# Gate and up products of an FFN by seven products of quarter blocks instead of eight, with precomputed weight sums and a serial background queue

## The chip, the cores and the metric

The kernel runs on one core of one Trainium2 chip. The metric is the device time of one execution in microseconds. The engines are TensorE (PE: matmuls and, as PEld, its weight loads), VectorE (DVE), ScalarE (ACT), GpSimd (POOL) and SyncE (SP, which here only issues DMAs).

## The reference

One inference step of one decoder layer with two parallel head groups, for a prompt of 2048 tokens with 16 meta tokens ahead of it and 8 running sequences of 8 new tokens each (64 sample tokens). Cut to what matters:

```
z = x @ w_in                       # q, k, v, conv path c, mLSTM v, output gate, input/forget gates
att = sliding-window attention(q, k, v)          # window 128, 8 query heads, 2 KV heads, sinks, ALiBi
h_m = mLSTM(silu(causal_conv(c)), ...)           # 4 heads of 128, chunk by chunk of 128 tokens
y   = concat([head_norm(att), head_norm(sigmoid(o_pre) * h_m)])
x1  = layer_norm(alpha * x + y @ w_out)          # 1024 features
ffn = (silu(x1 @ w_gate) * (x1 @ w_up)) @ w_down # 1024 -> 2816 -> 1024
out = layer_norm(alpha * x1 + ffn)
```

Besides the outputs y for prompt and sample tokens, the last keys and values, the conv state and the mLSTM state are returned. All data are float32.

## The kernel before, in words

Activations lie with features on the 128 partitions and tokens along the columns, so a product of a 128x128 weight block with up to 512 token columns is one matmul. To keep float32 accuracy at the faster matmul type, every operand is split into a rounded part and a remainder (`split`, lines 117 to 120: ACT rounds, line 111; DVE or Pool subtracts, line 120), and a product is three matmuls (`mm3`, lines 122 to 125: high by high, high by low, low by high).

The work has three stages. **First input projection** (lines 182 to 300): 17 token tiles times three column ranges of `w1a`, the results by tokens, stored to DRAM as `TM` and `TMS`. **Second input projection** (lines 904 to 992): five token groups of 424 or 426 columns times nine output tiles of `w1b` (six in the last group), convolution and the q/k maps, stored to DRAM as `FM`. **FFN stage** (lines 995 to 1248): five token groups of 384, 440, 440, 440 and 408 columns (`FF_GROUPS`). Of each group: the output projection `out_proj` (8 output tiles of 8 k-blocks), layer norm `ln1` with the split of its result into `x1`, then 22 feed-forward tiles of 128 features in `SLICES` of 5, 5, 6 and 6: for each tile `gate_up` (lines 1142 to 1161) makes two products of 8 k-blocks, gate and up, each in a PSUM bank of its own; ACT takes the tanh from the gate's bank, DVE makes t from it and multiplies with the up bank, and the result is split into `hh` and `hl`. After each slice `down` (lines 1163 to 1176) adds the slice's 8 output tiles to z. The next group's output projection and `ln1` stand within the last slice, `ln2` within the next group's first tiles.

Weights are loaded again for each group by `wtile` (line 998): SP loads 512 KB, ACT rounds, DVE (or Pool, one in eight of those with 8 k-blocks) subtracts. `wnext` keeps three ahead. Raw, high and low come in turn from one ring of 8 tiles of 1024 columns (`wpl`, line 151), so that the load of one waits until the ring comes round.

**Background.** Attention and mLSTM of the 16 prompt chunks, and of the sample tokens, are generators (`bg_attn`, line 484; `bg_ml`, line 628; `bg_sample_attn`, `bg_sample_ml`) that yield after each small step. A queue (lines 845 to 852) holds one entry for each chunk; `both` (line 835) takes one step of attention and one of mLSTM at a time, 12 double steps a chunk. `pace` gives out steps between the main products at a rate that brings a group's chunks to an end before its output projection needs them (`need`), and `bg_drain` runs what is left.

PSUM has eight banks: three for the main products (`gps`, line 75) and five for the background (`bps`, line 78).

What is written in this order is not the order of the engines: the kernel is built with `schedule_with_timeline_sim=True` (line 1347), where each engine's instructions are put in an order at build, by when their operands would be ready and by their place in the program. On the chip each engine then runs its list in that order.

Of the kernel before, what the change touches and what calls it, by code (L numbers as in the profile page):

```python
# [17 lines left out]
KD = 8  # L18
# [21 lines left out]
FF_GROUPS = [384, 440, 440, 440, 408]  # L40
FW = max(FF_GROUPS)
XW = max(IN_GROUPS + FF_GROUPS)
SLICES = [5, 5, 6, 6]
NLATE = 3
CZ = 3

# [3 lines left out]
def tile_hymba(  # L50
# [15 lines left out]

    cp = ctx.enter_context(tc.tile_pool(name="const", bufs=1))
# [4 lines left out]
    pg = ctx.enter_context(tc.tile_pool(name="pg", bufs=3, space=bass.MemoryType.PSUM))  # L72
    pb = ctx.enter_context(tc.tile_pool(name="pb", bufs=5, space=bass.MemoryType.PSUM))

    def gps(shape=None):
        return pg.tile(shape or [128, 512], F32, tag="g", name="gps")

    def bps(shape=None):
        return pb.tile(shape or [128, 512], F32, tag="b", name="bps")
# [42 lines left out]
    def mm3(out, wh, wl, xh, xl, start, stop):  # L122
        PE.matmul(out, lhsT=wh, rhs=xh, start=start, stop=False)  # L123
        PE.matmul(out, lhsT=wh, rhs=xl, start=False, stop=False)  # L124
        PE.matmul(out, lhsT=wl, rhs=xh, start=False, stop=stop)  # L125
# [25 lines left out]
    wpl = ctx.enter_context(tc.tile_pool(name="wpl", bufs=8, reuse_waits="tile"))  # L151
    xpl = ctx.enter_context(tc.tile_pool(name="xpl", bufs=22, reuse_waits="tile"))

    def w_tile(dt=F32R):
        return wpl.tile([128, KD, 128], dt, tag="w", name="w")

    def x_tile(dt=F32R):
        return xpl.tile([128, XW], dt, tag="x", name="x")

    def load_w(i):  # L160
        m = MT[i]
        if i < NEARLY:
            raw = ep.tile([128, KD, 128], F32, tag="wbr", name="wbr", bufs=1)
            hi, lo = w_tile(), w_tile()
        else:
            raw = b1["w"].tile([128, KD, 128], F32, tag="wbr", name="wbr", bufs=1)
            hi = b1["w"].tile([128, KD, 128], F32R, name=f"wbh{m}")
            lo = b1["w"].tile([128, KD, 128], F32R, name=f"wbl{m}")
        SP.dma_start(out=raw, in_=w1b[:, m, :].rearrange("p (k j) -> p k j", j=128))
        split("p" if i % 2 else "a", hi, lo, raw)  # L170
        wbh[m], wbl[m] = hi, lo
# [10 lines left out]
    with ExitStack() as s1:  # L182
        wp = s1.enter_context(tc.tile_pool(name="w1a", bufs=1, reuse_waits="tile"))
# [44 lines left out]
        start = [[f() for _ in CUT] for f in (gps, bps)]  # L228
# [14 lines left out]
        for i in range(NCH + 1):  # L243
# [11 lines left out]
            else:  # L255
                ps = []
                for c0, w in CUT:
                    xh, xl, n = xs[i]
                    p = (gps if flip[0] % 8 < 3 else bps)()
                    flip[0] += 1  # L260
# [4 lines left out]
            pa, pbk, pc = ps  # L265
            st = tp.tile([128, TMW], F32, tag="st", name="st", bufs=2)
# [36 lines left out]
    def gates():  # L303
# [35 lines left out]
        b = bps()  # L339
        PE.matmul(b[:, 0:NC4], lhsT=U, rhs=lf[:, 0:NC4], start=True, stop=True)  # L340
        bs = bps()
        PE.matmul(bs[0:NS, 0:4], lhsT=Us, rhs=lf[0:NS, sl], start=True, stop=True)
        bT = bps()
        PE.matmul(bT[0:NC4, 0:128], lhsT=lf[:, 0:NC4], rhs=U, start=True, stop=True)
        bTs = bps()
# [8 lines left out]
        aTs = bps()  # L354
# [112 lines left out]
    def att_rstd(o, w):  # L467

        sq = t2k("pt", [128, 512], 4)
        A.activation(out=sq[:, 0:w], in_=o[:, 0:w], func=AF.Square)  # L470
        sh, sl = (t2k("pt", [128, 512], 4, F32R) for _ in range(2))
# [5 lines left out]
        ve = t2k("pt", [128, 512], 4)  # L477
        V.tensor_scalar(out=ve[:, 0:w], in0=var[:, 0:w], scalar1=EPS, scalar2=None, op0=ALU.add)
        ry, tt = (t2k("pt", [128, 512], 4) for _ in range(2))
# [4 lines left out]
    def bg_attn(c):  # L484
# [19 lines left out]
        Pt = t2k("P", [128, 8, 256], 1)  # L504
# [30 lines left out]
        o = bps()  # L535
        halves = [(0, npv, 0), (nk - 128, 128, 1)]
        for c0, n, j in halves:
            ps = []
            for g in range(2):
# [3 lines left out]
                p = t2k("pt", [128, 512], 4)  # L543
# [60 lines left out]
    def bg_meta():  # L604
        km = t2k("fm", [128, 4, 128], 2)
        vm = t2k("vmo", [128, 4, 129], 1)
# [10 lines left out]
        S = t2k("S", [128, 4, 129], 2)  # L617
# [10 lines left out]
    def bg_ml(c):  # L628
# [4 lines left out]
        gw = t2k("gw", [128, 4, 2, 128], 1)  # L633
        vmo = t2k("vmo", [128, 1028], 1)
# [11 lines left out]
        gm = t2k("gm", [128, 4, 128], 1)  # L646
        G.affine_select(out=gm, in_=gw[:, :, 0, :], pattern=[[0, 4], [1, 128]], compare_op=ALU.is_ge,
# [8 lines left out]
        for h in range(4):  # L656
# [5 lines left out]
        V.tensor_tensor(out=gm.rearrange("p h t -> p (h t)"), in0=gm.rearrange("p h t -> p (h t)"), in1=sc,  # L662
                        op=ALU.mult)
        yield
        S = state["S"]
        Sn = t2k("S", [128, 4, 129], 2)
        nd = []
        for j in range(2):
            u = bps()
# [4 lines left out]
            for hh in range(2):  # L674
                h = 2 * j + hh
                V.scalar_tensor_tensor(out=Sn[:, h, :], in0=S[:, h, :], scalar=DEC[:, r0 + h:r0 + h + 1],
                                       in1=u[:, 129 * hh:129 * hh + 129], op0=ALU.mult, op1=ALU.add)
            yield
            x = bps([128, 2, 256])
            for hh in range(2):  # L680
                h = 2 * j + hh
                PE.matmul(x[:, hh, 0:129], lhsT=qs[:, h, :], rhs=S[:, h, :], start=True, stop=False)  # L682
                PE.matmul(x[:, hh, 0:129], lhsT=gm[:, h, :], rhs=vm[:, h, :], start=False, stop=True)
            nd.append(x[:, :, 0:129])
            yield
        state["S"] = Sn
        if c == NCH - 1:
            SP.dma_start(out=pS, in_=Sn)
        yield from mlstm_tail(nd, 128, ENM[:, r0:r0 + 4], o, 128 * c)

    def bg_sample_attn():
# [9 lines left out]
        o = bps()  # L701
        yield
        for hf in range(2):
# [10 lines left out]
            for g in range(2):  # L714
                pr = slice(64 * g, 64 * g + 64)
                tb = t2k("pt", [128, 192], 4)
# [6 lines left out]
                X = t2k("P", [128, 192], 1)  # L723
# [21 lines left out]
                ps = t2k("pt", [128, 256], 4)  # L745
# [22 lines left out]
    def bg_sample_ml():  # L768
        qm = t2k("fm", [128, 4, NS], 2)
        km = t2k("fm", [128, 4, NS], 2)  # L770
        sg = t2k("gw", [128, 4, 136], 1)
        vmo = t2k("vmo", [128, 1028], 1)
# [4 lines left out]
        SP.dma_start(out=vmo[0:NS], in_=TMS[0:NS, 128:TMW])  # L777
        vm = vmo[:, 0:516].rearrange("p (h e) -> p h e", h=4)
        o = vmo[:, 516:1028]
# [5 lines left out]
        gm = t2k("gm", [128, 4, NS], 1)  # L785
# [18 lines left out]
        nd = [bps([128, 2, 256]) for _ in range(2)]  # L804
        for h in range(4):
            pp = t2k("P", [128, 2, 8, 129], 1)
# [563 lines left out]
```

## Time and profile before

| what | us |
|---|---|
| median of 3 runs | 2508.75 (2508.75 to 2509.66) |
| the profiled execution | 2508.94 |
| its span, first to last instruction | 2507.1 |
| PE busy | 2444.7 |
| PEld busy (weight loads, beside PE) | 2267.2 |
| DVE busy | 1514.9 |
| ACT busy | 955.3 |
| POOL busy | 328.3 |

The mean granted TensorE clock was 0.989 of full speed. From the places of the first matmuls of each kind in the trace, the first input projection runs to 226 us, the second to 504 us, and the FFN stage from there to the end. How to read the lines: a group of instructions is `line engine operation out<-in shape xcount | busy us, mean ns of one | idle time of the engine before them, and what ended it`. In the order of time a line is `start us, us, engine line operation, out<-in, shape, count`; equal neighbours are merged. In the table of stretches each line gives busy time and count of PE, PEld, DVE, ACT and POOL, then the granted clock, the share of the DMA engines and GB/s. A matmul's record lasts until its result is written, and records of neighbours overlap; the step from one start to the next tells what a matmul costs.

### The profile page before, as it was taken

The page shows a single profiled execution, that of the slowest core. Times are in us where ns is not written, and L with a number is a line of the kernel's source. Part 1 is how long each engine was busy: PE and PEld are TensorE (multiplying, and loading weights), DVE is VectorE, ACT ScalarE, POOL GpSimd, SP SyncE. Part 2 cuts the span into 40 slices and gives each one's busy share as a digit, 9 for nine tenths or more (in the row PEclk, how much of TensorE's full clock was granted, in tenths as well). Part 3 has the DMA queues.
Part 4 walks back from the last instruction along what each step waited for, and adds up shares of the span by engine and source line. Part 5 has one row for each costly group of instructions (what it writes and reads, how often), then busy time and mean ns, then how long its engine had stood idle before and what let it go on. Part 6 is the DMA issues. An engine that isn't in the chain of part 4 may idle for free.

```text
span 2507.1 us, 34929 instructions
## 1 busy us (share of the span) xinstructions
PE 2444.7 (98%) x13135; PEld 2267.2 (90%) x13135; DVE 1514.9 (60%) x3129; ACT 955.3 (38%) x1730; POOL 328.3 (13%) x253
## 2 busy tenths in 40 slices
PE   8999999889999999999999999999999999999997
PEld 8999888788989989888999899989899999999997
DVE  6214466457786888656674976666775434764444
ACT  3112444335433444324333543343343323443332
POOL 1000000021000014210011500100420000420001
PEclk9999999998999999999999999999999999999998
DMA  7222534563444543554343353433344333343342
GB/s 234 89 90 85 173 119 131 132 207 117 144 130 126 160 146 94 175 159 144 120 137 121 106 188 122 140 119 107 109 142 133 117 111 121 104 143 114 118 127 77
DMA packets 197330, 327.89 MB, mean 131 GB/s; under 512 B 31010, under 2 KB 133498, under 8 KB 197146
## 3 DMA queue, kind: packets, MB, share of 16 engines
q1 hardware_dynamic: 170400, 294.29, 38.7%
q10 hardware_dynamic: 26762, 31.36, 3.6%
q8 instruction: 104, 1.70, 0.3%
q14 instruction: 64, 0.52, 0.1%
HBM read 281.59 MB, written 44.99 MB: 130 GB/s over the span
## 4 chain that ended last, share of the span: by engine, by line
PE 88%; DVE 4%; DMA 4%; ACT 1%; issue 1%; POOL 0%; SPq 0%; ACTq 0%; DVEq 0%; POOLq 0%
PE gps L123 25%; PE gps L125 24%; PE gps L124 24%; PE bps L123 2%; PE bps L125 2%; PE bps L124 2%; DMA w<-in_wo 1%; PE bps L513 1%; PE bps L549 1%; PE bps L542 1%; PE gps L937 1%; DVE w L120 1%; PE bps L682 1%; PE bps L655 1%; PE bps L672 1%
## 5 line engine op out<-in xcount | busy, mean ns | idle before, releaser
L123 PE MATMUL gps<-x,w 128*128 128x440 f32 (+4 forms) x2240 | 792.3, 358 | 11.1 <-DVE z L1075 5.6
L125 PE MATMUL gps<-x,w 128*128 128x440 f32 (+4 forms) x2240 | 797.9, 357 | 3.4 <-POOL w L120 2.7
L124 PE MATMUL gps<-x,w 128*128 128x440 f32 (+4 forms) x2240 | 794.0, 356 | 0.6 <-DVE x L1122 0.6
L111 ACT CAST w<-w 128x1024 fp32r<-128x1024 f32 (+2 forms) x423 | 400.6, 947 | 775.2 <-DMA w<-in_wd 271.8
L120 DVE TENSOR_TENSOR w<-w 128x1024 fp32r<-128x1024 f32 (+2 forms) x391 | 441.5, 1130 | 359.7 <-ACT w L111 185.4
L123 PEld LDWEIGHTS gps<-x,w 128*128 128x128 f32 x2240 | 422.4, 189 | 36.5 <-DVE z L1075 7.4
L125 PEld LDWEIGHTS gps<-x,w 128*128 128x128 f32 x2240 | 422.6, 189 | 23.3 <-POOL w L120 4.4
L124 PEld LDWEIGHTS gps<-x,w 128*128 128x128 f32 x2240 | 422.6, 189 | 18.4 <-DVE x L1122 0.9
L123 PE MATMUL gps<-hh,w 128*128 128x440 f32 (+2 forms) x880 | 314.8, 362 | 1.4 <-DVE z L1172 1.3
L125 PE MATMUL gps<-hh,w 128*128 128x440 f32 (+2 forms) x880 | 313.1, 357 | 0.0
L124 PE MATMUL gps<-hl,w 128*128 128x440 f32 (+2 forms) x880 | 312.5, 356 | 0.0
L123 PEld LDWEIGHTS gps<-hh,w 128*128 128x128 f32 x880 | 166.1, 189 | 11.9 <-issue 4.6
L124 PEld LDWEIGHTS gps<-hl,w 128*128 128x128 f32 x880 | 166.3, 189 | 8.1 <-issue 1.5
L125 PEld LDWEIGHTS gps<-hh,w 128*128 128x128 f32 x880 | 166.1, 189 | 7.4 <-issue 0.5
L120 POOL TENSOR_TENSOR w<-w 128x1024 fp32r<-128x1024 f32 x32 | 77.4, 2419 | 727.1 <-ACT w L111 475.2
L1172 DVE SCALAR_TENSOR_TENSOR z<-z,gps 128x440 f32<-128x440 f32 (+2 forms) x160 | 93.0, 589 | 69.1 <-PE gps L125 68.7
L111 ACT CAST hh<-hr 128x440 fp32r<-128x440 f32 (+2 forms) x110 | 60.0, 545 | 165.2 <-DVE hr L1158 165.0
L1158 DVE SCALAR_TENSOR_TENSOR hr<-ft,gps 128x440 f32<-128x440 f32 (+2 forms) x110 | 64.9, 590 | 81.3 <-PE gps L125 81.0
L1155 ACT ACTIVATE ft<-gps 128x440 f32<-128x440 f32 (+2 forms) x110 | 57.4, 522 | 113.1 <-PE gps L125 112.6
L120 DVE TENSOR_TENSOR hl<-hr,hh 128x440 fp32r<-128x440 f32 (+2 forms) x110 | 83.8, 762 | 27.6 <-ACT hh L111 27.3
L1066 POOL TENSOR_TENSOR zs<-zs,z 128x440 f32<-128x440 f32 (+2 forms) x58 | 80.0, 1379 | 102.0 <-DVE z L1075 66.3
L1156 DVE SCALAR_TENSOR_TENSOR ft<-ft,gps 128x440 f32<-128x440 f32 (+2 forms) x110 | 64.7, 588 | 46.4 <-ACT ft L1155 46.3
(338 smaller groups left out, 3111.0 us busy)
## 6 DMA issues: line engine op xcount, KB each, us to landing
w<-in_wg SPq DMA_DIRECT2D x110, 512.0 KB, 3.5
w<-in_wu SPq DMA_DIRECT2D x110, 512.0 KB, 3.5
w<-in_wd SPq DMA_DIRECT2D x80, 384.0 KB, 3.1
w<-in_wd SPq DMA_DIRECT2D x80, 320.0 KB, 2.9
w<-in_wo SPq DMA_DIRECT2D x40, 512.0 KB, 3.7
FM<-ev ACTq DMA_DIRECT2D x52, 213.0 KB, 1.9
TM<-st ACTq DMA_DIRECT2D x16, 578.0 KB, 3.7
vmo<-TM SPq DMA_DIRECT2D x16, 514.0 KB, 3.4
```

The costliest lines, as they stand in the source:

```text
L111: A.copy(out, src)
L120: return veng.tensor_tensor(out=lo, in0=src, in1=hi.bitcast(F32), op=ALU.subtract)
L123: PE.matmul(out, lhsT=wh, rhs=xh, start=start, stop=False)
L124: PE.matmul(out, lhsT=wh, rhs=xl, start=False, stop=False)
L125: PE.matmul(out, lhsT=wl, rhs=xh, start=False, stop=stop)
L513: PE.matmul(s[g][:, j, 0:nk], lhsT=x[r, 2 * tt + j, :], rhs=y[r, 0:nk], start=(i == 0), stop=(i == 2))
L542: PE.transpose(pt[0:n, 128 * t:128 * t + 128], Pt[:, 4 * g + t, c0:c0 + n], ident)
L1066: G.tensor_tensor(out=s[:, 0:w], in0=s[:, 0:w], in1=z[m][:, 0:w], op=ALU.add)
L1155: A.activation(out=t[:, 0:w], in_=pgt[:, 0:w], func=AF.Tanh, scale=0.5)
L1156: V.scalar_tensor_tensor(out=t[:, 0:w], in0=t[:, 0:w], scalar=1.0, in1=pgt[:, 0:w], op0=ALU.add, op1=ALU.mult)
L1158: V.scalar_tensor_tensor(out=hr[:, 0:w], in0=t[:, 0:w], scalar=0.5, in1=pu[:, 0:w], op0=ALU.mult, op1=ALU.mult)
L1172: V.scalar_tensor_tensor(out=zm, in0=zm, scalar=ALPHA if s == 0 else 1.0, in1=p[:, 0:w], op0=ALU.mult, op1=ALU.add)
```

## The change

**Gate and up.** The token groups become four pairs of half groups: `WH = [256, 256, 272, 272]`, so pairs of 512, 512, 544 and 544 columns (`W2`). For a pair of neighbouring feed-forward tiles (11 pairs) and for each of the two weights the product is that of a 2x2 block matrix A (two output tiles by two halves of k, each block 128 outputs by 4 k-blocks) with a 2x2 block matrix B (two halves of k by two half groups). It is made of seven products instead of eight, in the Winograd form of Strassen's scheme:

```
PROD = {"P1": ("A11", "B11"), "P2": ("A12", "B21"), "P3": ("S4", "B22"), "P4": ("A22", "T4"),
        "P5": ("S1", "T1"), "P6": ("S2", "T2"), "P7": ("S3", "T3")}
```

Each product is 4 k-blocks times three matmuls, 256 or 272 columns wide. S1 to S4 are sums of weight blocks, T1 to T4 sums of the blocks of x1. P6, P7 and P4 add onto P1's bank after it has been read, and P3 onto P5's:

```
if name == "P1":   A.copy(c1[:, a], p)
elif name == "P2": V.tensor_tensor(out=c1[:, a], in0=c1[:, a], in1=p, op=ALU.add)
elif name == "P6": A.copy(c1[:, b], p)
elif name == "P7": A.copy(c2[:, b], p)
                   V.tensor_tensor(out=c2[:, b], in0=c2[:, b], in1=S["ga"][:, a], op=ALU.add)
elif name == "P3": V.tensor_tensor(out=c1[:, b], in0=c1[:, b], in1=p, op=ALU.add); gated(S, 0)
elif name == "P4": A.copy(c2[:, a], p); gated(S, 1)
```

The order is, with P3 and P4 taken from the product set before: P1, P2, P3 (before), P6, P4 (before), P5, P7. P1's bank has two buffers, P2's and P5's one each. c1 and c2 lie in SBUF; `gated` takes tanh and products from there, at the full pair's width, and splits the result.

**Weight sums.** S1 to S4 of all 22 pairs are made once, in the two input-projection stages, and stored to a DRAM tensor `SW`; the FFN loads them from there for each group:

```
def sums(pool):
    for mt, src in enumerate((wg, wu)):
        for q in range(NPAIR):
            for o in (0, 256):
                a = ...tile([128, 2, 2, 256], F32, tag="sa", bufs=1); t = ...tile([128, 4, 256], F32, tag="st4", bufs=1)
                SP.dma_start(out=a, in_=src[:, 2*q:2*q+2, :]...[:, :, :, o:o + 256])
                for i, (x, y, op) in enumerate(...):       # four of them
                    G.tensor_tensor(out=t[:, i], in0=x, in1=y, op=op)
                A.dma_start(out=SW[:, NPAIR * mt + q, :, o:o + 256], in_=t)
                yield
```

There are 44 such steps. One follows each tile from the third on in the first stage (15), and each output tile in the second until they are used up (29).

**Sums of x1.** `ln1` now makes seven split operands of half the features and half the columns: B11, B21, T2, T1, T3, B22, T4. T1 and T3 are subtracted by Pool, T2 and T4 by DVE; the remainders of B22 and T4 are made by Pool.

**Weights of the FFN.** All come in blocks of 4 k-blocks (256 KB): for a group 154 for gate and up, 16 for the output projection, 48 for down (8 of them of 2 k-blocks). The ring has `NWB = 17` tiles of 512 columns; `LOOK = 5` blocks are asked for ahead. One in four (`WP = 4`) has its remainder made by Pool. `SLICES` is 4, 4, 4, 4, 6.

**Down and output projection** take 512 columns at once, or 544 as two of 272. In the last group `down` of the last slice goes over the first half and then the second, and each half has its own `ln2`.

**PSUM and background.** Four banks (tags ga twice, gb, gc) serve the main products, two `b` and two `bo` the background. `both` gives way to `chain`: attention of a chunk, then its mLSTM, 19 single steps; mLSTM now makes its outputs from the state before it updates the state in place, and several work tiles share one buffer `P`. As the first pair needs 512 tokens, four chunks instead of three have to be done before the FFN stage. Steps are given out after each of the seven products; while a group's `ln2` runs, a step of it is taken after P3 and P5 instead.

```
-        queue.append((e, e, 12, both(bg_attn(c), bg_ml(c))))
+        queue.append((e, e, 19, chain(bg_attn(c), bg_ml(c))))
```

**Small things.** The conv state of the sample tokens is loaded and stored in one DMA each by SP instead of four each on ACT's queue; late tiles of q are written through another buffer; the buffers for temporaries are renumbered (`FTB = 7`, `PTB = 3`).

More of the change, by code (lines that the diff above doesn't have):

```diff
@@ L39 @@
 IN_GROUPS = [426, 426, 426, 426, 424]
[L40 to L43, printed above, removed]
+WH = [256, 256, 272, 272]
+W2 = [2 * w for w in WH]
+F0 = [sum(W2[:i]) for i in range(len(W2))]
+HW = max(WH)
+FW = 2 * HW
+SLICES = [4, 4, 4, 4, 6]
+NPAIR = NFF // 2
 NLATE = 3
 CZ = 3
+NWB = 17
+PTB = 3
+FTB = 7
+LOOK = 5
+WP = 4
+NFIRST = 12
+LSTEP = [2, 1, 1, 1, 1, 1, 2, 2]
 @with_exitstack
@@ new lines, in ln2 @@
+        def ln2(g, cc, fast=False):
+            z = P[g]["z"]
+            for c in cc:
+                ry = yield from norm(z, c, P[g]["zs"], bps, fast)
+                for k in range(KD):
+                    scale(z, k, c, ry, Q_L2G)
+                    A.activation(out=z[k][:, c], in_=z[k][:, c], func=AF.Identity,
+                                 bias=Q[:, Q_L2B + k:Q_L2B + k + 1])
+                    (SP if fast else A).dma_start(out=yT[:, k, F0[g] + c.start:F0[g] + c.stop], in_=z[k][:, c])
+                    if k == KD // 2 - 1 and not fast:
+                        yield
+                yield
@@ new lines, in tile_hymba, with after, down, fn @@
+        pend, rate = [None], [0.0]
+        def after(name):
+            if pend[0] is not None:
+                if name in ("P3", "P5") and next(pend[0], 0) == 0:
+                    pend[0] = None
+            else:
+                pace(rate[0])
+        def down(g, s, m, cc, zs, adds, then=None):
+            j0, n = sum(SLICES[:s]), SLICES[s]
+            parts = [(k, min(4, n - k)) for k in range(0, n, 4)]
+            def fn(*wb):
+                z, h = P[g]["z"], P[g]["h"][:n]
+                for c in cc:
+                    p = gps()[:, 0:c.stop - c.start]
+                    for (k, nn), w in zip(parts, wb):
+                        product(p, w, [(hh[:, c], hl[:, c]) for hh, hl in h[k:k + nn]], k == 0, k + nn == n)
+                    zm = z[m][:, c]
+                    V.scalar_tensor_tensor(out=zm, in0=zm, scalar=ALPHA if s == 0 else 1.0, in1=p,
+                                           op0=ALU.mult, op1=ALU.add)
+                    if zs and m < adds:
+                        add_to(P[g]["zs"], z, m, c)
+                if then is None:
+                    pace(rate[0])
+                else:
+                    then()
+            item(fn, *[(wd[:, m, 128 * (j0 + k):128 * (j0 + k + nn)], nn) for k, nn in parts])
@@ L1252, in _consts @@
+        run()
 def _consts():
```

623 lines of the change are left out of this document (362 added, 261 removed).

## The prediction

> **What bounds the kernel now.** I read the page's first and fourth parts, then busy time by stage, then single matmuls in the order of time, then the groups of instructions by shape.
>
> ```profile
> span 2507.1 us, 34929 instructions
> PE 2444.7 (98%) x13135; PEld 2267.2 (90%) x13135; DVE 1514.9 (60%) x3129; ACT 955.3 (38%) x1730; POOL 328.3 (13%) x253
> ...
> PE 88%; DVE 4%; DMA 4%; ACT 1%; issue 1%; POOL 0%; SPq 0%; ACTq 0%; DVEq 0%; POOLq 0%
> ```
>
> TensorE is busy 98% of the span and makes 88% of the chain that ended last; it is idle for 2507.1 - 2444.7 = 62 us in all. A change that takes matmul time away is worth that time, as long as no other engine becomes late. Busy time by stage (the two input-projection stages, then the FFN stage from 504 us), and in two stretches of 100 us:
>
> ```profile
> 0.00:226.00 226.00, 219.34 (x1224) 215.69 (x1225) 72.23 (x172) 51.05 (x90) 23.72 (x42) 1.00 0.39 128
> 226.00:504.00 278.00, 269.79 (x1414) 234.91 (x1412) 163.58 (x453) 125.81 (x287) 11.70 (x12) 0.99 0.48 136
> 504.00:2507.00 2003.00, 1955.57 (x10501) 1816.63 (x10500) 1279.08 (x2505) 778.41 (x1354) 292.88 (x199) 0.99 0.42 130
> ...
> 800.00:900.00 100.00, 99.91 (x605) 92.24 (x605) 82.01 (x216) 46.94 (x102) 8.99 (x6) 1.00 0.50 153
> 1400.00:1500.00 100.00, 98.76 (x533) 88.24 (x532) 84.34 (x171) 52.36 (x101) 24.43 (x18) 1.00 0.47 152
> ```
>
> The columns are PE, PEld, DVE, ACT, POOL, then the granted clock (0.99 to 1.00: no throttle to win back) and DMA. In the FFN stage DVE is busy 1279 of 2003 us. Where it is busiest, 82 and 84 of 100 us, TensorE still reaches 99.9 and 98.8: up to there DVE does not hold it.
>
> **TensorE's part of the change.** What a matmul costs is its step to the next one, since records overlap. Steps at 440, 384 and 408 columns, then a run of score matmuls at 256 columns and one of 128:
>
> ```profile
> 1900.04 0.37 PE L125 MATMUL gps<-x,w 128*128 128x440 f32 x1
> ...
> 1902.44 0.36 PE L125 MATMUL gps<-x,w 128*128 128x440 f32 x1
> ```
> ```profile
> 640.13 0.34 PE L125 MATMUL gps<-hh,w 128*128 128x384 f32 x1
> ...
> 641.70 0.34 PE L125 MATMUL gps<-hh,w 128*128 128x384 f32 x1
> ```
> ```profile
> 2250.00 0.35 PE L124 MATMUL gps<-hl,w 128*128 128x408 f32 x1
> ...
> 2251.85 0.35 PE L125 MATMUL gps<-hh,w 128*128 128x408 f32 x1
> ```
> ```profile
> 1134.59 0.98 PE L513 MATMUL bps<-kt,qt 64*128 64x256 f32 x12
> 1134.82 0.52 PE L513 MATMUL bps<-kt,qt 64*128 64x256 f32 x6
> ...
> 1135.29 0.28 PE L513 MATMUL bps<-kt,qt 64*128 64x256 f32 x2
> ```
> ```profile
> 1135.82 0.39 PE L655 MATMUL bps<-fm 128*128 128x128 f32 x2
> ...
> 1136.16 0.50 PE L655 MATMUL bps<-fm 128*128 128x128 f32 x3
> ```
>
> Twelve steps at 440 columns take 2.40 us: 200 ns. Nine at 384 take 1.57: 174. Ten at 408 take 1.85: 185. So a column costs 26/56 = 0.46 ns. The score matmuls run as pairs in the two halves of the rows; after the first, four steps take 1135.29 - 1134.82 = 0.47 us, 118 ns with a new weight load each; I take 119 for the view's rounding. At 272 columns that is 119 + 16 x 0.46 = 126. The L655 run (128 columns, two passes of an exact float32) steps at 0.34/3 = 113 with a full 128x128 load each: a load that nothing hides better cannot be much longer than that.
>
> Gate and up before: 22 tiles x 2 matrices x 8 k x 3 = 1056 matmuls a group, so 1056 x (174 + 3 x 200 + 185) ns = 1013 us. After: 11 pairs x 2 x 7 products x 4 k x 3 = 1848 a group, two groups at 256 and two at 272: 3696 x (119 + 126) ns = 906 us. **Term: -107 us.** Seven products for eight alone would be -127; the rest is that short matmuls cost 0.465 ns a column for 0.455. Bounds of the step: 113 (the L655 load) gives 3696 x (113 + 120) = 861, 45 us better; 119 + 12 = 131 gives 995, where the term is nearly gone.
>
> Down and output projection keep their matmuls, 528 + 192 = 720 a group: before 720 x 959 ns = 690 us. After, at 512 columns 200 + 72 x 0.46 = 233 ns, and 544 as two of 272: 720 x 2 x (233 + 252) = 698. **Term: +8.** Background matmuls, the late tiles and the norms stay, one background chunk moving from the FFN stage into the second input stage; both stages are TensorE's, so that is nothing in sum.
>
> **What lies beside it.** Rows for the other engines, by shape:
>
> ```profile
> L120 DVE TENSOR_TENSOR w<-w 128x1024 fp32r<-128x1024 f32 x231 | 292.0, 1265 | 195.1 <-ACT w L111 131.7 <-PE gps L124 37.0 <-issue 14.3
> L120 DVE TENSOR_TENSOR w<-w 128x768 fp32r<-128x768 f32 x80 | 83.5, 1043 | 92.9 <-PE gps L124 60.5 <-ACT w L111 26.3 <-issue 3.2
> L120 DVE TENSOR_TENSOR w<-w 128x640 fp32r<-128x640 f32 x80 | 66.0, 826 | 71.8 <-PE gps L124 36.0 <-ACT w L111 27.5 <-issue 5.4
> ...
> L120 DVE TENSOR_TENSOR hl<-hr,hh 128x440 fp32r<-128x440 f32 x66 | 50.2, 761 | 17.0 <-ACT hh L111 16.6
> ...
> L136 DVE SCALAR_TENSOR_TENSOR pt<-pt 128x512 f32<-128x512 f32 x48 | 33.0, 688 | 0.7
> ...
> L120 DVE TENSOR_TENSOR x<-x 128x440 fp32r<-128x440 f32 x24 | 14.3, 611 | 10.1 <-ACT x L111 10.1
> ...
> L120 DVE TENSOR_TENSOR kt<-kt 128x256 fp32r<-128x256 f32 x15 | 6.3, 418 | 1.7 <-PE bps L722 1.7
> ```
> ```profile
> 858.83 0.69 DVE L136 SCALAR_TENSOR_TENSOR pt<-pt 128x512 f32<-128x512 f32 x1
> 859.43 0.48 DVE L518 CUSTOM_DVE_ANT_0 P<-bps,C,R 128x256 f32<-128x256 f32 x1
> ```
> ```profile
> L526 ACT ACTIVATE P<-P,mx 128x256 f32<-128x256 f32 x120 | 59.3, 496 | 22.6 <-DVE mx L523 21.0 <-issue 1.6
> ...
> L526 ACT ACTIVATION_READ_ACCUMULATOR P<-P,mx 128x1 f32 x128 | 23.9, 187 | 0.0
> ...
> L111 ACT CAST qt<-qt 128x512 fp32r<-128x512 f32 x16 | 9.9, 618 | 17.5 <-PE bps L513 16.0 <-DMA qt<-FM 1.4
> ```
> ```profile
> L120 POOL TENSOR_TENSOR w<-w 128x1024 fp32r<-128x1024 f32 x32 | 77.4, 2419 | 727.1 <-ACT w L111 475.2 <-PE gps L125 123.5 <-PE gps L124 74.1
> ...
> L644 POOL TENSOR_TENSOR wkv<-vmo,WK 128x516 f32<-128x516 f32 x16 | 19.5, 1219 | 100.7 <-DMA vmo<-TM 76.6 <-PE bps L622 24.1
> ```
>
> On DVE a 512-wide operation lasts 0.69 us but the next starts 0.60 after it, so 0.09 of each is overlap; a 256-wide one then takes 0.42 - 0.09 = 0.33. Count for DVE in the FFN stage. Weight splits: before 391, 441 us (406 without overlap); after 4 x (154 + 16 + 48) + 6 = 878 half-size blocks, a quarter of them on Pool, 658 x 0.60 = 395: -11. New additions of the products into SBUF: 88 product sets x 3 x 0.33 = +87. Splits of the seven token operands and their sums, 28 half-width operations a group: +37. Evictions and gating: fewer but wider, within 20 either way. Pool's splits rise from 77 to 220 x 1.22 = 268 us, and DVE and Pool get in each other's way: hl takes 761 where x, of one operation and width, takes 611. Of those 191 us I charge DVE 50, bounds 0 and 191. The sum is 1279 - 11 + 87 + 37 + 50 = 1442, at most 1583, of some 1900 us: 76 to 83%, within the 82 to 84% above. So DVE does not become the bound on the average.
>
> [...]
>
> ACT splits 878 blocks at 0.62 = 544 us for 426, and copies 88 x 4 quarters at about 0.4: it stays under 60%.
>
> **New waits.** What shrinks is slack. A gate/up bank now has to be read within two products of 12 x 119 = 1.43 us after its own, 2.9 us, before P5, P3, P6 or P7 may write over it or add to it; before, three banks of 24 x 200 ns gave 9.6. Behind a late addition on DVE stand the next splits, and the matmuls that wait for both. Weight blocks:
>
> ```profile
> w<-in_wg SPq DMA_DIRECT2D x110, 512.0 KB, 3.5
> ...
> w<-in_wd SPq DMA_DIRECT2D x80, 320.0 KB, 2.9
> ...
> TM<-st ACTq DMA_DIRECT2D x16, 578.0 KB, 3.7
> ...
> fm<-FM SPq DMA_DIRECT2D x32, 256.0 KB, 3.4
> ```
>
> With 17 tiles in the ring a block's load starts when the block six earlier is used up, five products (7.1 us) ahead of its use; load 3.4 (bounds 2.9 and 3.5), cast 0.62, subtraction 0.69 or on Pool 1.22 leave 1.9 to 2.4 us. Before: 9.6 - 3.5 - 1.05 - 1.27 = 3.8. The engines' order is laid down at build by readiness (above, a score operation stands between two steps of one background chain), so waits are mostly filled, and before only 47 us were idle in this stage. If half of the 88 product sets lose one DVE operation, 44 x 0.69 = **+30 us**; bounds 0 and the first rival's 140.
>
> Weight sums: 44 steps of four 256-wide additions on Pool, about 0.7 each (half of the 516-wide row, plus a fixed part), 123 us, in stages where Pool has 35 of 504 us to do. What hides them is that idle Pool. They queue 44 stores on ACT, each waiting for Pool, with that tile's eviction behind it. A step can't be shorter than its additions and the store of the step before, 4 x 0.7 + 3.7 = 6.5 us (one buffer each); the second stage's tiles come every 278/42 = 6.6 us, the first's every 13. Barely hidden: **+5**, bounds 0 and, if additions take 1.2 us beside DVE, 29 x 2 = 58. Each transition to a next group splits 28 operand quarters more, and DVE has (8 subtractions, 8 scalings, 8 evictions, 12 weight splits) x 0.60 + 28 x 0.33 = 31 us of work there, under 8 down tiles of 18 x 233 ns = 33 us; with the start **+14**. The last norm is 272 wide for 408: **-4**.
>
> **Sum.** 2507 - 107 + 8 + 30 + 5 + 14 - 4 = 2453. The profiled execution took 2508.94, 1.8 over its span and 0.2 over the median of the runs, 2508.75: **2455 us**.
>
> **Rivals.** *The background chains hold the products (slower).* Three chains of a chunk have rows here:
>
> ```profile
> L592 DVE TENSOR_SCALAR qs<-qs,dn 128x128 f32<-128x128 f32 x64 | 18.8, 354 | 0.4
> ...
> L581 DVE SCALAR_TENSOR_TENSOR qs<-bps,dn,vmo 128x128 f32<-128x128 f32 x64 | 18.1, 345 | 0.5
> ...
> L585 DVE BATCH_NORM_STATS2 dn<-qs 128x6 f32<-128x128 f32 x64 | 13.9, 278 | 0.0
> ```
>
> The exponentials with their accumulator reads take ACT 8 x (0.50 + 0.19) = 5.5 us, the nine Newton operations on 512 columns DVE 9 x 0.60 = 5.4, the mLSTM tail at least 4 x (0.35 + 0.35 + 0.28) = 3.9. Against 2.9 us of slack they leave 1 to 2.6 us bare each, and both the eviction and the next blocks' splits can be caught: up to 10 us a chunk, with twelve chunks and two sample parts 140 us instead of 30: 2565. It decides from (107 - 8 - 5 - 14 + 4)/12 = 7 us a chunk. For it: serial chains with two banks instead of five. Against: the filled order and the 84% stretch.
>
> *The weight load is not hidden at 256 columns.* The score pairs load half the rows each; if a full load adds 12 ns to a step, 3696 x (131 + 138) = 994 and the time is 2543; in the first score step it is bare, 1134.82 - 1134.59 = 230 ns, a far end. Against: L655's 113.
>
> [...]
>
> *No new waits.* All stays filled and the step is nearer 113: 2455 - 30 - 14 - 25 = about 2385 to 2410.
>
> *The sums don't hide.* ACT falls behind by 2 us in 29 tiles: 2455 + 53 = 2508, no change.
>
> **How the numbers follow.** About 0.2% (5 us) is what a measurement here can tell. Forecast 0.60, own range 2425 to 2490; no new waits 0.15; sums bare 0.05; chains 0.14; load 0.06. Faster: 0.60 + 0.15 and 0.02 of the sums case, 0.77; same: the rest of that case and a mild load case, 0.04; slower 0.19. Leaving out the slowest half of the chains' case and the fastest fringe gives 2395 to 2545.
>
> **What would show it.** Gate/up matmuls at 256 and 272 columns stepping at 119 and 126 ns (113 or 131 would settle the load); TensorE idle near 100 us, its waits going to DVE and ACT at c, w; DVE some 75% of the FFN stage; Pool about 25%; the second input stage no longer than 295 us with its extra chunk. Wrong if TensorE's idle time in the first three FFN groups passes 120 us, or the step passes 131.

## The result, and the profile after

The changed kernel takes 3044.44 us (median of 4 runs, 3043.24 to 3046.59) against 2509.2 us before: ratio 1.2133, 95% interval 1.2112 to 1.2154. It is 21% slower; the prediction had 2455 us and its slowest rival 2565. No run of the study beats the kernel before.

From the page of the changed kernel: span, busy time, the shares of the chain that ended last, the cast and the subtraction of a weight split (L133, L142), the additions of the sums (L195), and the time from issue to landing of a weight block and of a store of the sums.

```profile
span 3044.8 us, 44281 instructions
...
PE 2595.5 (85%) x16021; PEld 2296.1 (75%) x16021; DVE 1779.2 (58%) x3971; ACT 1182.6 (39%) x2594; POOL 571.0 (19%) x566
...
PE 4%; DVE 2%; issue 1%; ACT 1%; POOL 0%; DMA 0%; DVEq 0%; ACTq 0%; POOLq 0%
...
L133 ACT CAST w<-w 128x512 fp32r<-128x512 f32 x894 | 526.2, 608 | 432.0 <-DMA w<-in_wd 151.9
L142 DVE TENSOR_TENSOR w<-w 128x512 fp32r<-128x512 f32 (+1 forms) x783 | 571.3, 737 | 121.3 <-ACT w L133 109.8
...
L195 POOL TENSOR_TENSOR st<-sa 128x256 f32<-128x256 f32 x88 | 67.1, 783 | 224.1 <-DMA SW<-st 217.4
...
w<-SW SPq DMA_DIRECT2D x352, 256.0 KB, 2.8
...
SW<-st ACTq DMA_DIRECT2D x44, 512.0 KB, 5.4
```

TensorE is now idle 3044.8 - 2595.5 = 449 us, where it was idle 62. Yet no engine is full: VectorE has 58%. The chain shares add up to 8%: here the chain could be followed only a short way back, so this part of the page is not used. Busy time by stage (the columns are PE, PEld, DVE, ACT, POOL, granted clock, DMA share, GB/s): the two input stages, a stretch between them and the FFN stage that the kernel before did not have, the FFN stage, and in it the last group's products, which carry no background work:

```profile
0.00:226.00 226.00, 220.38 (x1224) 216.11 (x1225) 72.15 (x176) 49.66 (x92) 64.74 (x104) 1.00 0.60 196
226.00:516.00 290.00, 271.12 (x1339) 231.26 (x1338) 159.77 (x402) 117.80 (x276) 107.18 (x128) 0.98 0.67 219
516.00:582.50 66.50, 32.52 (x150) 23.15 (x148) 45.91 (x150) 21.59 (x55) 3.44 (x3) 0.66 0.47 148
582.50:3044.80 2462.30, 2071.45 (x13312) 1825.60 (x13312) 1501.37 (x3245) 993.56 (x2173) 395.62 (x331) 0.94 0.40 118
...
2506.00:2958.00 452.00, 382.35 (x2646) 352.31 (x2646) 232.53 (x431) 180.74 (x376) 59.36 (x51) 0.95 0.39 112
```

Where TensorE does run, it runs as forecast. Two uninterrupted pieces of the timeline, at 256 and at 272 columns:

```profile
1449.67 0.28 PE L147 MATMUL gps<-x,w 128*128 128x256 f32 x1
...
1450.73 0.28 PE L147 MATMUL gps<-x,w 128*128 128x256 f32 x1
...
2413.06 0.28 PE L146 MATMUL gps<-x,w 128*128 128x272 f32 x1
...
2415.18 0.28 PE L145 MATMUL gps<-x,w 128*128 128x272 f32 x1
```

Nine steps take 1.06 us (118 ns), seventeen take 2.12 (125 ns). So the loss is time between matmuls. I measure it in one way throughout: each matmul's step to the next, less the usual step of its shape (the 35th percentile), summed over a stretch; call it lost time. In the FFN stage (from 582.5 us; before from 504.5) the usual steps add up to 1752 us after and 1831 before, and the lost time is 702 after (533 in gaps over 150 ns, 169 in smaller ones) and 163 before. The balance to the last matmul is then: start of the stage +78, steps -79, lost time +539: +538 us.

What TensorE waits for at a gate, up, down or output bank, from the view of waits (us in total, times, longest), split weight blocks (w) and, the third line, an eviction (z). After:

```profile
PE gps L147 <- DVE w L142: 135.0, 195, 6.7
PE gps L145 <- ACT w L133: 106.4, 105, 7.1
PE gps L145 <- DVE z L1314: 26.1, 42, 2.3
...
PE gps L147 <- POOL w L142: 19.4, 28, 3.8
```

Before:

```profile
PE gps L125 <- POOL w L120: 2.7, 3, 1.4
...
PE gps L123 <- ACT w L111: 2.0, 1, 2.0
...
PE gps L125 <- DVE w L120: 0.6, 1, 0.6
```

Split weight blocks make 261 us of waits after and 5 before. Few of these blocks are late from memory. I followed each wait back through the trace to the last thing that was waited for: 172 of the 261 us go back to an operation in ScalarE's, VectorE's or GpSimd's list that waited for a main product, 32 to one that waited for a background product, and 33 to a cast that waited for its own block to land. One case of the first kind, in the last group, from the timeline of the changed kernel (start, duration, then idle time before and its releaser):

```profile
2644.47 3.63 SPq L1061 DMA_DIRECT2D w<-SW  x2
...
2654.20 0.39 ACT L1275 COPY ft<-gps 128x272 f32<-128x272 f32 x1 [0.59 <-PE gps L147]
2654.49 1.14 ACT L133 CAST w<-w 128x512 fp32r<-128x512 f32 x2
...
2655.94 0.29 PE L146 MATMUL gps<-x,w 128*128 128x272 f32 x1
2656.08 0.44 DVE L1277 TENSOR_TENSOR ft<-ft,gps 128x272 f32<-128x272 f32 x1 [1.68 <-PE gps L147]
2656.43 0.69 DVE L142 TENSOR_TENSOR w<-w 128x512 fp32r<-128x512 f32 x1
...
2657.18 0.39 PE L147 MATMUL gps<-x,w 128*128 128x272 f32 x1 [0.95 <-DVE w L142]
```

Numbering blocks in the order of loads, casts and subtractions, the one loaded at 2644.47 (2.8 us to land) is cast at 2654.49 and subtracted at 2656.43. It lay there for 7 us. ScalarE stood before the copy of a product that had not ended; then came copy, cast, and on VectorE, idle for 1.68 us, an addition that waited for the next product, and only behind it the subtraction, whose cast had ended 1.3 us before. TensorE got its block 1.1 us late. Over the last group a block's cast starts 8.0 us after its load is issued on average, 5 us after it has landed. The instruction lists that the build lays down say the same (an eviction is the operation that takes a product out of its bank): past the first 40 blocks 141 of 747 subtractions on VectorE stand behind the eviction of the product just before their use and 195 behind the one two before; in the kernel before, none and 43 of 353, at products of 4.8 us instead of 1.43.

### The profile page after: what moved, and what is told of

It reads as the page before. It is cut to its first block, busy times and chain, and to the rows that moved or that the text cites. A ratio compares the mean times of both kernels' runs of the same rounds, so it can differ in the third digit from the quotient of the medians.

```text
span 3044.8 us, 44281 instructions
## 1 busy us (share of the span) xinstructions
PE 2595.5 (85%) x16021; PEld 2296.1 (75%) x16021; DVE 1779.2 (58%) x3971; ACT 1182.6 (39%) x2594; POOL 571.0 (19%) x566
## 5 line engine op out<-in xcount | busy, mean ns | idle before, releaser
L147 PE MATMUL gps<-x,w 128*128 128x272 f32 (+4 forms) x3008 | 936.4, 314 | 137.3 <-DVE w L142 120.8
L145 PE MATMUL gps<-x,w 128*128 128x272 f32 (+4 forms) x3008 | 926.5, 312 | 137.1 <-ACT w L133 101.7
L146 PE MATMUL gps<-x,w 128*128 128x272 f32 (+4 forms) x3008 | 908.7, 303 | 13.8 <-DVE x L142 12.3
L147 PEld LDWEIGHTS gps<-x,w 128*128 128x128 f32 x3008 | 591.0, 197 | 205.3 <-DVE w L142 172.7
L145 PEld LDWEIGHTS gps<-x,w 128*128 128x128 f32 x3008 | 592.3, 198 | 192.0 <-ACT w L133 125.3
L133 ACT CAST w<-w 128x512 fp32r<-128x512 f32 x894 | 526.2, 608 | 432.0 <-DMA w<-in_wd 151.9
L142 DVE TENSOR_TENSOR w<-w 128x512 fp32r<-128x512 f32 (+1 forms) x783 | 571.3, 737 | 121.3 <-ACT w L133 109.8
L146 PEld LDWEIGHTS gps<-x,w 128*128 128x128 f32 x3008 | 594.3, 198 | 27.9 <-DVE x L142 18.0
L142 POOL TENSOR_TENSOR w<-w 128x512 fp32r<-128x512 f32 (+1 forms) x111 | 143.5, 1292 | 1477.9 <-ACT w L133 980.8
L145 PE MATMUL gps<-h,w 128*128 128x272 f32 (+1 forms) x1056 | 353.5, 335 | 30.3 <-DVE z L1314 18.9
L147 PE MATMUL gps<-h,w 128*128 128x272 f32 (+1 forms) x1056 | 347.6, 332 | 19.7 <-DVE w L142 14.2
L146 PE MATMUL gps<-h,w 128*128 128x272 f32 (+1 forms) x1056 | 344.5, 326 | 0.3 <-DVE h L142 0.3
L145 PEld LDWEIGHTS gps<-h,w 128*128 128x128 f32 x1056 | 202.3, 192 | 58.9 <-issue 15.7
L147 PEld LDWEIGHTS gps<-h,w 128*128 128x128 f32 x1056 | 200.8, 191 | 47.5 <-DVE w L142 25.5
L1314 DVE SCALAR_TENSOR_TENSOR z<-z,gps 128x272 f32<-128x272 f32 (+1 forms) x240 | 124.4, 518 | 181.6 <-PE gps L147 180.6
L146 PEld LDWEIGHTS gps<-h,w 128*128 128x128 f32 x1056 | 202.4, 192 | 14.0 <-DVE h L142 0.5
L133 ACT CAST h<-ft 128x512 fp32r<-128x512 f32 (+1 forms) x88 | 55.7, 633 | 172.7 <-DVE ft L1250 172.5
L142 DVE TENSOR_TENSOR x<-x 128x426 fp32r<-128x426 f32 (+3 forms) x72 | 51.4, 714 | 99.7 <-ACT x L133 79.9
L195 POOL TENSOR_TENSOR st<-sa 128x256 f32<-128x256 f32 x88 | 67.1, 783 | 224.1 <-DMA SW<-st 217.4
L1115 POOL TENSOR_TENSOR zs<-zs,z 128x512 f32<-128x512 f32 (+2 forms) x58 | 79.7, 1376 | 145.4 <-DVE z L1128 78.7
```

The lines of the kernel that those rows point to most:

```text
L133: A.copy(out, src)
L142: return veng.tensor_tensor(out=lo, in0=src, in1=hi.bitcast(F32), op=ALU.subtract)
L145: PE.matmul(out, lhsT=wh, rhs=xh, start=start, stop=False, **kw)
L146: PE.matmul(out, lhsT=wh, rhs=xl, start=False, stop=False, **kw)
L147: PE.matmul(out, lhsT=wl, rhs=xh, start=False, stop=stop, **kw)
L195: G.tensor_tensor(out=t[:, i], in0=x, in1=y, op=op)
```

## The experiments

Theory: **order in the lists**. ScalarE and VectorE take their lists strictly in turn, and the lists put a block's cast and subtraction behind evictions of products one or two before its use. The rows above agree with the first part: VectorE stood idle for 1.68 us, though for the last 1.0 us of that the subtraction behind the addition had its cast. Rivals: the serial background work holds the products; banks are reused too soon; VectorE or GpSimd has too much to do. Times are medians of 4 runs where nothing else is said, with the ratio to the kernel before, whose median was 2509.3 to 2509.4 us wherever a ratio is given.

**Evictions queued behind later splits.** Issue order alone, with K = 2 or 3:

```
+ with issue_after(cast of block b+K), issue_after(subtraction of block b+K):
      A.copy(c1[:, a], p)          # and every other eviction of block b's product
```

> The changed kernel with one thing more: in the lists of ScalarE and VectorE each product's eviction is queued behind the cast and the subtraction of the weight block two products later (issue order alone; no wait, no work added or taken away). Theory (list order): the blocks land about 8 us before their use, but 141 of some 750 subtractions stand behind the eviction of the product just before their use, 195 behind the one two before, and TensorE stands while eviction and subtraction run one after the other. Then idle time in the four FFN groups (gaps 470 us, and 150 us more in steps lengthened by the lower clock) falls by a third to two thirds: 2650 to 2850 us. Rival (background work, serial and in two banks, holds the products): the order of evictions and splits does not matter, 3000 to 3080 us. Rival (bank reuse: a bank has to be read within 2.9 us): evictions come later here, so no faster, 3040 to 3150 us.

> As the run with two products, but each eviction is queued behind the splits of the block three products later. Theory (list order): more of the idle time goes, 2500 to 2750 us, faster than with two. Rival (background): 3000 to 3080. Rival (bank reuse): evictions later still, slower than with two products and than the changed kernel, over 3050.

K = 2: 2891.8 us, ratio 1.1504 (1.1474 to 1.1534); K = 3: 2872.9, 1.1439 (1.1410 to 1.1469). So 153 and 172 us come back from order alone. That is outside the windows of both rivals, but less than the theory expected. The waits of the second kernel show what took their place:

```profile
PE gps L149 <- DVE w L144: 47.9, 58, 5.7
PE gps L147 <- DVE z L1330: 39.2, 47, 4.8
PE gps L147 <- ACT w L135: 27.3, 19, 3.9
PE gps L147 <- DVE ft L1297: 23.7, 16, 4.1
```

Waits for split blocks fall from 261 to 80 us; waits for evictions (z of the down products, ft of the gate and up products) rise from 38 to 98. So in these lists what is put ahead makes the other late.

**One link of the split left out.**

```
# no subtraction:              # no cast:          (both with NWB = 16 for 17, to make room for the block kept)
A.copy(hi, raw)                V.tensor_tensor(out=lo, in0=raw, in1=hi_once, op=subtract)
return hi, lo_once             return hi_once, lo
```

> The changed kernel without the FFN stage's weight subtractions: loads and casts stay, and one low-order block made once serves all products (left out: 893 subtractions on VectorE and GpSimd; the low-order part of the weights is not right). Theory (list order): the subtraction's place in VectorE's list costs TensorE more than half of its waits (L147 121 us, weight loads 173 us beside), the casts' place in ScalarE's list stays: 2650 to 2850 us. Rival (background chains): 2980 to 3050. Rival (weight blocks come too late from memory): the loads stay, 3000 to 3050.

> The changed kernel without the FFN stage's weight casts: loads and subtractions stay, one rounded high-order block made once serves all products and all subtractions (left out: 893 casts on ScalarE; the products are not the right ones). Theory (a chain over two in-order lists: ScalarE's copy of a product, behind it the cast of a block needed a product later, behind that VectorE's subtraction, 0.38 + 0.62 + 0.74 us and more against a product of 1.43): either link taken away brings the chain under a product, 2600 to 2800 us. Rival (VectorE's own list, its additions and background steps, holds the subtractions wherever their input is): 2930 to 3040.

Without subtractions 2582.3 us, ratio 1.0273 (1.0241 to 1.0305), without casts 2649.2, 1.0559 (1.0543 to 1.0574): 462 and 395 us less than the changed kernel; the first is faster than the theory's window, the second lies in it. The engine rows of their pages, first without casts:

```profile
PE 2441.1 (92%) x16021; PEld 2233.0 (84%) x16021; DVE 1779.1 (67%) x3971; ACT 697.6 (26%) x1701; POOL 582.6 (22%) x566
```

Without subtractions:

```profile
PE 2414.9 (94%) x16021; PEld 2220.3 (86%) x16021; DVE 1242.3 (48%) x3189; ACT 1172.9 (45%) x2594; POOL 406.5 (16%) x455
```

The run without casts is the sharper one. VectorE does all its 1779 us of work in it, as in the changed kernel, and ScalarE was not full before (39%), and still TensorE goes from 85 to 92%. So it is not VectorE's load. My reading is the chain through both engines: copy of a product, cast behind it, subtraction behind that, 0.38 + 0.61 + 0.74 = 1.73 us and the hand-overs, against a product of 1.43 us; either link away, the rest fits under a product.

That the length of the chain decides is argued, not shown, because these two edits change the lists too. I counted places from the order in the traces, with numbers close to the build's: subtractions on VectorE behind the eviction of the product just before or two before their use are 130 and 198 of 748 in the changed kernel, 1 and 49 with K = 3, and 16 and 24 without casts. Casts on ScalarE behind the copies of these two products are 12 and 304 of 854 in the changed kernel and 2 and 28 without subtractions. With one link gone the build puts the other earlier, and evictions are waited for about as long as before (41 us without casts, for 38). The two runs show that the two-step split is what holds TensorE; they do not tell the chain's length from its place in the lists.

**The additions left out.**

```
- V.tensor_tensor(out=c1[:, a], in0=c1[:, a], in1=p, op=ALU.add)    # P2; also P5's and P3's
```

> The changed kernel without the three additions per product set on VectorE that read P2's, P5's and P3's banks (left out: 264 additions of 256 or 272 columns, so the gated values lack these products). They are 264 x 0.44 = 116 us of VectorE's time and each waits for a running product. Theory (list order): weight subtractions stop standing behind them, only ScalarE's copies still wait for products; well over 116 us comes back, 2700 to 2870. Rival (VectorE has too much to do, wherever it stands): at most the 116 us, 2930 to 3000.

2980.7 us, ratio 1.1868 (1.1847 to 1.1889): 64 us, the rival's size; the theory's number was wrong. That VectorE's own additions hold the subtractions, as in the timeline above, is the lesser part. Split-block waits that go back to an operation of VectorE fall from 102 to 18 us, those that go back to one of ScalarE rise from 69 to 84: the copies on ScalarE remain in this kernel.

**Subtractions moved between VectorE and GpSimd.**

```
- WP = 8                 # one in 8 on GpSimd
+ WP = 4                 # one in 4; or 100000: none; with the order K = 3: 2, and none
```

> The changed kernel with the inner WP at 4, so that a quarter of the weight subtractions is on GpSimd, as the prediction took it to be (it is an eighth). Theory (list order): subtractions that stand behind the eviction of the product just before go from 141 to 101 of VectorE's list, 113 x 0.74 = 84 us leave VectorE: 2950 to 3010. Rival (the missing quarter is what made the prediction wrong): under 2700.

> The changed kernel with no weight subtraction on GpSimd (783 of 894 were on VectorE, now all). Theory (GpSimd's subtractions hold VectorE up and come late themselves: a quarter there cost 31 us against an eighth): 3000 to 3035. Rival (list order alone: subtractions behind the eviction of the product just before go from 141 to 197, and VectorE gets 82 us more to do): 3055 to 3110.

> The kernel with evictions queued behind the splits of the block three products later (2873 us), and every second weight subtraction on GpSimd in place of every eighth: 336 x 0.69 = 232 us leave VectorE, GpSimd takes 336 x 1.29 = 433 us more. Theory (what the order left over is VectorE's in-order list filling up between evictions, background and splits): 2650 to 2790. Rival (what is left is banks and background chains): 2840 to 2890. Rival (GpSimd holds VectorE up while it runs, or its 1.29 us come too late): 2880 or more.

> The kernel with evictions queued behind the splits of the block three products later (2873 us), with no weight subtraction on GpSimd. Theory (GpSimd's subtractions cost more than they take over: half there cost 50 us against an eighth): 2820 to 2865. Rival (VectorE's load): 2880 to 2950.

A quarter on GpSimd: 3074.1 us (median of three executions; the fourth, the profiled one, took 13178 us, so no trace of this kernel is read), 1.2246 (1.2225 to 1.2266), 30 slower, where 35 to 95 faster was expected. None: 3056.8, 1.2185 (1.2167 to 1.2203), 12 slower. With K = 3, half on GpSimd 2923.4, 1.1642 (1.1594 to 1.1691), 51 slower; none 2872.0, 1.1451 (1.1434 to 1.1468), the same as one in eight (2872.9). All four lie outside the theory's windows. So VectorE's load is not what is short, and relieving it through GpSimd beyond one in eight makes things worse. The rows of VectorE's subtraction with K = 3, first with none on GpSimd, then with half:

```profile
L144 DVE TENSOR_TENSOR w<-w 128x512 fp32r<-128x512 f32 x854 | 622.7, 737 | 192.6 <-ACT w L135 188.4
```
```profile
L144 DVE TENSOR_TENSOR w<-w 128x512 fp32r<-128x512 f32 x447 | 366.7, 821 | 157.0 <-ACT w L135 119.6 <-issue 26.5 <-DMA w<-in_wg 2.1
```

On the mean each remaining one lasts 84 ns longer, 447 x 84 ns = 38 us, and GpSimd's own last 1.34 us, nearly a whole product. The mean mixes two kinds of subtraction, which the last section takes apart.

**The serial background in the kernel before.**

```
- queue.append((e, e, 12, both(bg_attn(c), bg_ml(c))))
+ queue.append((e, e, 19, chain(bg_attn(c), bg_ml(c))))
```

and, with and without it, a first group that needs four chunks of background ahead of the FFN stage, as the changed kernel's does:

```
- FF_GROUPS = [384, 440, 440, 440, 408]
+ FF_GROUPS = [440, 440, 440, 440, 352]
```

> The kernel before with its two background chains of a chunk one after the other instead of alternating (19 steps a chunk in place of 12), its five banks and all else as before. Theory (list order): products of 4.8 us cover it; only what has to be drained ahead of the FFN stage costs, 2509 to 2560 us. Rival (the serial background work holds the products): 2600 us or more.

> The kernel before with serial background chains and with its first FFN group as wide as the others (440, 440, 440, 440, 352), so that four chunks in place of three must be done ahead of the FFN stage, as in the changed kernel. Theory (a serial chunk takes about 70 us of latency and the fourth is ready last): the FFN stage starts 45 to 75 us later than the 513 us of the run with chains alone, and 2575 to 2625 us in all. Rival (a chunk moved costs nothing in sum, as the prediction had it): 2535 to 2555.

> The kernel before with its first FFN group as wide as the others (440, 440, 440, 440, 352), so that four chunks must be done ahead of the FFN stage; chains alternate as before. Theory (what is waited for ahead of the stage comes back as background work that the stage no longer has, as with serial chains, where the same step took 2545 to 2522): 2485 to 2510 us. Rival (the fourth chunk's wait is a loss): 2525 to 2560.

All three are within 2% of the kernel before, and clear of it by their intervals. Chains alone 2544.8 us, 1.0135 (1.0115 to 1.0154): +35; the FFN stage starts at 513.0, 8 us later, and loses 29 us more (192 for 163). With the wide first group 2522.1, 1.0046 (1.0031 to 1.0061): the stage starts at 533.9, 21 us later, but loses only 153 us in it and has a chunk less to do, so more than that comes back: the run is 23 us faster than with chains alone. With alternating chains 2518.9 (5 runs), 1.0034 (1.0020 to 1.0049), start at 531.3. The last two lie outside my windows, the theory's and the rival's. The changed kernel's stage starts at 582.5: by analogy with these runs the chains explain 8 us of its 78 and the fourth chunk about 21; the other 49 are left to what it has besides, two pairs of banks, single buffers for the state and for the shared tile, and the sums. Which of them was not tried.

**Background out of the way.**

```
- bg_drain(need(0))          # what the first group needs
+ bg_drain(P0 + 128 * 13)    # 13 of 16 chunks ahead of the FFN stage, sample parts last
```

> The changed kernel with 13 of 16 chunks of background done ahead of the FFN stage and the sample parts last, so that the first two FFN groups carry next to no background work; nothing is left out, and the time is far longer (the chunks run bare, some 9 x 68 us), so only the groups are read. Time lost per group over the matmuls' own steps was 172 and 199 us. Theory (the place of the splits in the lists makes the stalls, with or without background): 130 to 180 us in each of the two groups, as in the last. Rival (background steps make them): under 90.

> The same with evictions queued behind the splits of the block three products later, where the first two groups lost 144 and 169 us. Theory (what the repaired order leaves in these groups is background steps that stand in the same lists and wait for their own inputs): 55 to 90 us in each of the two, as in the last group (74). Rival (it is something of the groups themselves, the transition or banks): 130 or more.

One run each, 3283.6 and 3027.3 us, read by groups alone. The second group, first to last product, in windows: the changed kernel, K = 3, then the background early, in the two orders. (The columns are as above; the count beside PE shows the background's matmuls go.)

```profile
1278.30:1808.50 530.20, 434.79 (x2655) 372.26 (x2654) 336.69 (x772) 215.81 (x475) 63.74 (x51) 0.92 0.43 128
```
```profile
1252.00:1754.00 502.00, 420.19 (x2654) 366.71 (x2653) 338.08 (x782) 219.35 (x489) 66.49 (x54) 0.93 0.45 135
```
```profile
1557.40:2002.50 445.10, 358.14 (x2226) 311.65 (x2225) 227.33 (x369) 168.73 (x338) 48.65 (x40) 0.95 0.41 122
```
```profile
1480.00:1842.90 362.90, 328.64 (x2226) 304.17 (x2225) 226.14 (x379) 174.94 (x350) 51.74 (x42) 0.95 0.49 149
```

Lost time in these windows: 178 us, with the order 151, with the background away 141, with both 59. In the first group it is 146, 123, 122 and 44. Each remedy alone gives 23 to 37 us, both give 102 and 119. In the build's order one window is inside the theory's 130 to 180 us and one (122) just under it; with the order 59 is inside its 55 to 90 and 44 under it, both far from the rival's 130. I read it so: one list has two kinds of instructions that wait, evictions and background steps, and as long as either stands ahead of a split, TensorE waits about as long. Lost time by whole groups, from a group's first product to the next group's:

```
                          group 1   2     3     4 (no background)
changed kernel               172   199   150   163
order, K = 2                 154   175   112    84
order, K = 3                 144   169   118    74
without additions            165   177   140   132
without casts                 73    94    58    59
without subtractions          57    77    39    44
```

In the fourth group, without background, order alone takes 163 to 74, near the 59 without casts: there the theory holds by itself. In the others it needs the background gone as well. Where a link of the split is left out, the first two groups lose only 57 to 94 us with all their background in place, so most of what the background costs there it costs through the splits.

## Why the prediction was wrong, point by point

- **The step that failed is the term for new waits**, +30 us with bounds 0 and 140, on the ground that "the engines' order is laid down at build by readiness (...), so waits are mostly filled". It measured +539 (702 of lost time for 163, the transitions between groups included). The slack beside it was worked out for one block alone: load 3.4, cast 0.62, subtraction 0.69 inside 7.1 us. All of that was right, the load was even quicker (2.8), and the slack of about 2 us was there and more, since the blocks lay there for 5 us on average. What was missing is that each link starts when its engine's list reaches it, and that is when a product of the near past has ended. The quantity I would compare now is eviction + cast + subtraction with one product: after, 0.38 + 0.61 + 0.74 = 1.73 us against 1.43; before, 0.59 + 1.05 + 1.27 = 2.91 us against 4.8. The runs fit it, but none varied the product's length with the chain kept, so it is not shown to be the limit.
- **"DVE does not become the bound on the average"** was right and no answer. I forecast 1442 us in the FFN stage, at most 1583; it has 1501. The cover I cited, stretches at 84% with TensorE at 99%, came from products of 4.8 us. With products of 1.43, the early-background window in the build's order has VectorE busy 227 of 445 us, 51%, and still loses 141.
- **Weight splits, a quarter on GpSimd**: a misreading. An inner WP = 8 stands over the module's 4, so it was 111 of 894, not 220. It did not make the error: the run with a quarter is 30 us slower.
- **The matmul term, -107, and down and output, +8**: right. Steps measured 118 and 125 ns for 119 and 126. Of all matmuls in the stage the usual steps fell by 79. The main products alone fell by 108, against a forecast of 99; the difference lies in the background, where the 35th percentile of score matmuls that run in pairs moved from 14 to 118 ns and makes a poor usual step.
- **The chunk that moves ahead, "nothing in sum"**: wrong by place. The second input stage did stay under my 295 us (290), but 66.5 us follow it in which TensorE has 32.5 us of work at a granted clock of 0.66, because the background that the first group needs ends last. The stage starts 78 us later. In the kernel before, with serial chains, the fourth chunk costs 21 us there and more than that is given back; with alternating chains the wide first group leaves 10 us.
- **The sums, +5**: the size was about right, the reckoning was not. The first input stage kept its 226 us, and the second is 8 us longer than with chains alone (282), a chunk more in it included. But the additions took 0.78 us for 0.7 and the stores 5.4 for 3.7, so that a step is 4 x 0.78 + 5.4 = 8.5 us and longer than a tile's 6.6. GpSimd waits 217 us for the stores, and ScalarE, whose list issues them, stands 62 us for GpSimd's sums. What that adds to the 49 us above was not tried.
- **Last norm, -4**: right; from the last down matmul to the end 23.9 us became 19.8.
- **Rivals**: the background chains were the nearest, but priced at up to 10 us a chunk as a mechanism by itself; in the kernel before they cost 35 us in all, and in the changed kernel the background is one of two causes that cover each other. The load at 256 columns is hidden (118 ns), and no run shows the 12 ns that its rival put on a step. "No new waits" could not have been further off.
- **The signs to look for** were well chosen: idle time over 120 us in the first three groups was to prove it wrong, and the gaps there add up to 128 + 152 + 115 = 395.

That the lower clock adds to the loss is read from its records alone: inside the half-speed spells of the FFN stage, steps with TensorE not idle are 108 us longer than usual in sum, for 15 before. The clock was not tried by itself.

## What to carry to other kernels

Before shortening a unit of work on the bound engine, look up where in each engine's list the links of its preparation stand (here cast and subtraction, between evictions), and write down the chain of in-order hand-overs beside one unit; landing times, buffer counts and busy shares did not show it here. When a stall has two causes in the same queue, removing one shows a fraction of its worth (here 23 to 37 us each, 102 and 119 together), so test them together as well as one by one. Work that must be complete before a stage starts was not moved for nothing here (66.5 us ahead of the stage), though it fitted by sums: ask which chain ends last.

## What the runs showed of the hardware

**Subtractions on VectorE and GpSimd held each other up.** A stretch of the run with K = 3 and half of the subtractions on GpSimd, both engines in the order of time:

```profile
2613.16 0.69 DVE L144 TENSOR_TENSOR w<-w 128x512 fp32r<-128x512 f32 x1
...
2613.60 1.40 POOL L144 TENSOR_TENSOR w<-w 128x512 fp32r<-128x512 f32 x1 [2.38 <-ACT w L135]
...
2613.84 0.44 DVE L1297 TENSOR_TENSOR ft<-ft,gps 128x272 f32<-128x272 f32 x1
2614.42 1.13 DVE L144 TENSOR_TENSOR w<-w 128x512 fp32r<-128x512 f32 x1
```

The second VectorE subtraction begins while GpSimd's runs, lasts 1.13 us for 0.69, and ends 0.55 us after GpSimd's end. The addition ahead of it, with one input in PSUM, takes its usual 0.44. In this trace 95 VectorE subtractions begin while one of GpSimd's runs: nine in ten end 546 to 552 ns after it, however late they began, and they last 1.20 us on the mean; the 230 that meet no GpSimd instruction last 0.69. The other way round, GpSimd's subtractions that begin while VectorE's runs last 1.40 us (median), for 1.29 where they meet nothing on VectorE. So in this trace a subtraction that meets one takes as long as if it waited for the end of the one that began first. The mean of 0.82 looks mild only because few of them meet, and the 50 of 191 us that the prediction charged VectorE came from such a mean (761 ns of hl for 611 of x).

**The granted clock fell to half in spells, not all of them at a pause of TensorE.** The changed kernel's trace holds four spells at half speed between 2503.7 and 2595.8 us, around the first products of the last group. The first begins in a pause of TensorE of 3.1 us, the third at the end of one of 2.65. The second (at 2541.3) and the fourth (at 2585.6) have no pause above 1.6 us in the 15 us ahead of them. Whether a pause sets the clock back is not shown here.
